# A low score product padded from 64 to 128 rows, in a two-block fp32 kernel

## The chip, the cores and the metric

The kernel runs on one core of one Trainium2 chip. The metric is the device time of one launch in microseconds (us), taken as the median of several runs. All tables of weights are laid out on the host beforehand, without arithmetic, and every product, norm and softmax runs on the core.

## The reference, cut to what matters

The reference is two transformer blocks over 1024 tokens of width 1024, all in fp32. The first block has a sliding-window attention and a gated FFN. The second block has two attentions side by side, and the change sits in the scores of both:

```
# stick-breaking attention, 8 heads of width 64
z = einsum('bhqd,bhkd->bhqk', q, k) * scale          # masked to s < t
log_1mb = where(mask, log_sigmoid(-z), 0)
a = where(mask, exp(log_sigmoid(z) + reverse_cumsum(log_1mb) - log_1mb), 0)
out = a @ v

# differential attention, 4 heads, two score maps of width 64 each
p1 = softmax(where(mask, q1 @ k1.T * scale, -1e30))
p2 = softmax(where(mask, q2 @ k2.T * scale, -1e30))
out = (p1 - lam * p2) @ v
```

After the attentions come gates, a projection with a residual, and a second gated FFN.

## The kernel before, in words

**Precision.** Each fp32 operand is split into a high part, rounded to the format that TensorE takes in one pass (fp32r), and a low part, the rest. A product of two split operands is three products that add up in one PSUM tile: high by high, high by low, low by high. Low by low is left out.

**Scores.** A head of width 64 fills only half of TensorE's 128 rows, so the kernel stacks. `k_stack` (line 1702) loads k's high part into 64 partitions of a tile and k's low part into the other 64. `q_stack` (line 1710) fills a tile `qs` of two slots, for 256 query positions: slot 0 holds q's high part twice, once in each half; slot 1 holds q's low part, in that half alone in which k's high part lies. `scores` (line 1719) then needs two products: slot 0 against all 128 rows of k's tile (line 1723, high by high and high by low at once), and slot 1 against the 64 rows of k's high part (line 1726, low by high). Where the piece touches the diagonal, a third product adds the mask (line 1729). Here q is what is loaded into the array as weights (128 columns of one query tile), and k streams through it, 128 to 512 columns wide.

A stick-breaking call of `scores` handles one pair of q and k. A differential call handles the two score maps together: line 1723 twice, line 1726 twice, line 1729 twice. The second map has its halves swapped (`up` is 1), so that its line 1726 uses rows 64 to 127 while the first map's uses rows 0 to 63.

**The order of the work.** A head's queries come in 8 tiles of 128, and its keys, up to the diagonal, in one or two pieces of at most 512 columns: 12 units for a head, so 96 stick-breaking units and 48 differential ones. Each unit is a tick of a plan written out by hand (`Plan.run`, line 187 on). A stick-breaking unit's scores stand in tick t, its softplus, exponentials and running sum on ScalarE (ACT) and VectorE (DVE) in t+1 and t+2, its transposes on TensorE (line 1735) in t+2, the split of the transposed weights (lines 296 and 297, tile `phl`) in t+3, and its product with v (line 1836) in t+4. A differential unit follows the same pattern (its product with v is line 1976). Between these, `Fill.run` (line 128 on) puts in the projections of the second block and its gates, as products of 512 columns (line 152). Their weights come through SyncE's (SP's) one DMA queue, are rounded on ACT or DVE and split on DVE or GpSimd (POOL, line 102). Every engine works through its own list in order; the lists' order does not depend on what happens at run time.

`q_stack` is called in the slot "load" of a tick, 3 ticks ahead of the tile's first use in a stick-breaking head and 2 ticks ahead in a differential one. The tile `qs` has 4 buffers; there are 64 loads of it, 32 for each attention, three DMAs each.

Of the kernel before, what the change touches and what calls it, by code (L numbers as in the profile page):

```python
# [10 lines left out]
F32 = mybir.dt.float32  # L11
# [183 lines left out]
class Kern:  # L195
# [1401 lines left out]
    def block2_attn(self, stack):  # L1597
        nc = self.nc
# [111 lines left out]
        def q_stack(Q, j, g, cs, up=0):  # L1710

            dst = self.t(pl, [P, 2, 256], "qs", bufs=4, dt=F32R)
            r = slice(g * 64, g * 64 + 64)
            nc.sync.dma_start(dst[:64, 0].bitcast(F32), Q[j][r, cs])
            nc.sync.dma_start(dst[64:, 0].bitcast(F32), Q[j][r, cs])
            nc.sync.dma_start(dst[up * 64 : up * 64 + 64, 1].bitcast(F32), Q[4 + j][r, cs])
            return dst

        def scores(qk, c0, w, mask):

            z = [self.ps("sc")[:, :w] for _ in qk]
            for i, (q, k) in enumerate(qk):
                nc.tensor.matmul(z[i], q[:, 0], k[:, c0 : c0 + w], start=True, stop=False)
            for i, (q, k) in enumerate(qk):
                r = slice(i * 64, i * 64 + 64)
                nc.tensor.matmul(z[i], q[r, 1], k[r, c0 : c0 + w], start=False, stop=mask is None)
            if mask is not None:
                for x in z:
                    nc.tensor.matmul(x[:, w - P : w], self.conr["ident"], self.conr[mask], start=False, stop=True)
            return z  # L1730
# [33 lines left out]
        def stick_head(h):  # L1764
# [21 lines left out]
            for qt in range(NT):  # L1786
                L = (qt + 1) * P
                if qt % 2 == 0:
                    def loadq(qt=qt):
                        H["q", qt] = H["q", qt + 1] = q_stack(SQ, j, g, slice(qt * P, qt * P + 256))  # L1790
                    if h + qt:
                        at(max(0, len(ticks) - 3), "load", loadq)
                    else:
                        loadq()
                for c0, w in reversed(cut(L)):
                    stick_unit(H, h, qt, c0, w, L)

        def stick_unit(H, h, qt, c0, w, L):
# [4 lines left out]
            def score():  # L1803
                q = H["q", qt][:, :, (qt % 2) * P : (qt % 2) * P + P]
                (u["z"],) = scores([(q, H["k"])], c0, w, "stm" if c0 + w == L else None)
# [52 lines left out]
        def diff_head(h):  # L1858
            H = {}

            def load():
                needs(44)
                for s in range(2):
                    H["k", s] = k_stack(DK, h, s, s)
                for i in range(2):
                    H["v", i] = self.t(pl, [P, T], "kv", bufs=6, dt=F32R)
                    nc.sync.dma_start(
                        H["v", i].bitcast(F32), DV[h][:, i * 4 : i * 4 + 4, :].rearrange("p t d -> p (t d)"))

            at(len(ticks) - 5, "load", load)  # L1870
            for qt in range(NT):
                L = (qt + 1) * P
                if qt % 2 == 0:
                    def loadq(qt=qt):
                        for s in range(2):
                            H["q", qt, s] = H["q", qt + 1, s] = q_stack(DQ, h, s, slice(qt * P, qt * P + 256), s)
                    at(len(ticks) - 2, "load", loadq)
                diff_tile(H, h, qt, cut(L), L)
# [62 lines left out]
        def diff_unit(H, Q, t, qt, ch, nch, c0, w, L):  # L1941
            u = {}

            def score():
                qk = [(H["q", qt, s][:, :, (qt % 2) * P : (qt % 2) * P + P], H["k", s]) for s in range(2)]
                u[0], u[1] = scores(qk, c0, w, "dam" if c0 + w == L else None)
# [402 lines left out]
```

## Time and profile before

| what | value |
|---|---|
| median of 3 runs | 2677.01 us (2676.76 to 2686.59) |
| the profiled execution: its time | 2672.5 us |
| the profiled execution: first to last instruction (span) | 2670.7 us |
| PE (TensorE) busy | 2597.1 us, 97% of the span |
| DVE busy | 1870.3 us, 70% |
| ACT busy | 1158.2 us, 43% |
| POOL busy | 660.9 us, 25% |
| mean granted TensorE clock | 0.99 |

A busy PE in this profile is not a PE at its peak: matmuls overlap, and their ends are modelled. What one of them costs is read from the distance between the starts of two that follow each other. The second block's attentions run from about 1154 us to 1800 us of the span.

### The profile page before, as it was taken

How to read it: one execution, taken by the hardware profiler on the slowest of the kernel's cores; microseconds unless marked ns; L12 is line 12 of the kernel's file. 1: busy time of each engine (PE TensorE's matmuls, PEld its weight loads, DVE VectorE, ACT ScalarE, POOL GpSimd, SP SyncE). 2: the span in 40 equal slices, each digit the busy share in tenths (PEclk: the TensorE clock that was granted, in tenths of full speed). 3: DMA queues.
4: the chain of work that ended last, by engine and by line, in shares of the span. 5: the costliest groups of instructions: out<-in, count | busy, mean ns of one | idle time of the engine just before them, and what ended most of it. 6: DMA issues, size and time to landing. Idle time of an engine off the chain costs nothing. (4 is left out here: it accounts for less than half of the span.)

```text
span 2670.7 us, 34280 instructions
## 1 busy us (share of the span) xinstructions
PE 2597.1 (97%) x12078; PEld 2085.7 (78%) x12078; DVE 1870.3 (70%) x2836; ACT 1158.2 (43%) x2080; POOL 660.9 (25%) x571
## 2 busy tenths in 40 slices
PE   9999999999999999899999999999999999999999
PEld 8766787788778778677777777787887788887887
DVE  5688867887887566726788777775636767776654
ACT  3444525433333334526766765554316222323442
POOL 4323254002343332311255111110001003331501
PEclk8999999999999999999999999999999999999999
DMA  6243575434555886346344343336634446565973
GB/s 257 80 158 123 162 264 193 175 137 169 200 171 192 301 285 216 126 128 198 92 131 126 123 132 116 112 105 230 240 142 144 158 140 209 171 215 189 369 243 133
DMA packets 224604, 470.84 MB, mean 176 GB/s; under 512 B 26672, under 2 KB 73904, under 8 KB 224432
## 3 DMA queue, kind: packets, MB, share of 16 engines
q1 hardware_dynamic: 224432, 468.65, 52.3%
q8 instruction: 95, 1.56, 0.2%
q14 instruction: 77, 0.63, 0.1%
HBM read 331.18 MB, written 137.36 MB: 175 GB/s over the span
## 5 line engine op out<-in xcount | busy, mean ns | idle before, releaser
L1353 POOL TENSOR_TENSOR raw<-raw,raw 128x512 f32<-128x512 f32 x78 | 141.3, 1811 | 417.0 <-DMA raw<-in_w_down 210.8
L152 PE MATMUL mm<-ah,wh 128*128 128x512 f32 x544 | 219.8, 404 | 1.8 <-DVE gb L606 1.8
L152 PE MATMUL mm<-ah,wl 128*128 128x512 f32 x544 | 219.3, 403 | 0.0
L152 PE MATMUL mm<-al,wh 128*128 128x512 f32 x544 | 219.0, 403 | 0.0
L102 POOL TENSOR_TENSOR wl<-raw,wh 128x1024 fp32r<-128x1024 f32 x44 | 106.5, 2421 | 399.3 <-DVE wh L101 159.8
L1216 DVE TENSOR_TENSOR W<-W 128x1024 f32<-128x1024 f32 x132 | 129.9, 987 | 14.5 <-DMA W<-in_w_up 12.5
L152 PEld LDWEIGHTS mm<-ah,wh 128*128 128x128 f32 x544 | 102.6, 189 | 22.5 <-issue 2.6
L152 PEld LDWEIGHTS mm<-ah,wl 128*128 128x128 f32 x544 | 102.6, 189 | 20.7 <-issue 2.5
L152 PEld LDWEIGHTS mm<-al,wh 128*128 128x128 f32 x544 | 102.7, 189 | 20.1 <-issue 2.2
L152 PE MATMUL mm<-wl,ah 128*128 128x512 f32 x256 | 102.4, 400 | 1.0 <-DVE wl L102 0.8
L152 PE MATMUL mm<-wh,al 128*128 128x512 f32 x256 | 103.2, 403 | 0.0
L152 PE MATMUL mm<-wh,ah 128*128 128x512 f32 x256 | 102.3, 400 | 0.0
L1152 PE MATMUL sc<-s,wh 128*128 128x512 f32 x344 | 100.6, 394 | 1.6 <-DVE u L1288 1.5
L1820 DVE TENSOR_TENSOR_SCAN w<-sc,w,w 128x383 f32<-128x383 f32 (+3 forms) x96 | 97.4, 1015 | 3.4
L297 DVE TENSOR_TENSOR wl<-rb,wh 128x1024 fp32r<-128x1024 f32 x52 | 77.1, 1483 | 23.7 <-ACT wh L296 19.4
L1507 PE MATMUL sc<-wh,ah 128*128 128x512 f32 x272 | 91.2, 389 | 0.0
L297 DVE TENSOR_TENSOR phl<-tp,phl 128x512 fp32r<-128x512 f32 (+2 forms) x144 | 78.3, 544 | 15.6 <-ACT phl L296 15.5
L1152 PE MATMUL mm<-ah,wh 128*128 128x512 f32 x236 | 79.7, 400 | 8.8 <-DVE wt L1105 5.0
L1816 DVE SCALAR_TENSOR_TENSOR w<-sc,w 128x384 f32<-128x384 f32 (+3 forms) x96 | 53.2, 554 | 45.7 <-ACT w L1815 45.4
L296 ACT CAST phl<-tp 128x512 fp32r<-128x512 f32 (+2 forms) x144 | 67.9, 472 | 34.5 <-PE tp L1735 34.2
L244 POOL TENSOR_SCALAR rs<-ss 128x1 f32<-128x1 f32 x40 | 16.5, 413 | 264.4 <-ACT xn L312 243.3
L1152 PE MATMUL mm<-al,wh 128*128 128x512 f32 x236 | 77.9, 399 | 3.9 <-ACT s L1172 3.9
(561 smaller groups left out, 7603.9 us busy)
## 6 DMA issues: line engine op xcount, KB each, us to landing
W<-in_w_up SPq DMA_DIRECT2D x88, 512.0 KB, 4.5
adaw<-in_ada_w SPq DMA_DIRECT2D x64, 256.0 KB, 3.0
raw<-in_w_in SPq DMA_DIRECT2D x31, 512.0 KB, 3.7
Fa<-g SPq DMA_DIRECT2D x44, 256.0 KB, 2.6
Fb<-g SPq DMA_DIRECT2D x44, 256.0 KB, 2.9
tw<-in_w_down SPq DMA_DIRECT2D x20, 512.0 KB, 5.3
rb<-in_w_down SPq DMA_DIRECT2D x40, 256.0 KB, 5.3
raw<-Fa SPq DMA_DIRECT2D x18, 512.0 KB, 4.9
```

Source lines behind the costliest of these rows:

```text
L102: (nc.vector if i in self.vec else nc.gpsimd).tensor_tensor(out=wl, in0=raw, in1=wh.bitcast(F32), op=ALU.subtract)
L152: kern.last_mm = kern.nc.tensor.matmul(ps, l, r, start=k == 0 and i == 0, stop=k == KT - 1 and i == 2)
L244: self.nc.gpsimd.tensor_scalar(out=out, in0=ss, scalar1=1.0 / n, scalar2=EPS, op0=ALU.mult, op1=ALU.add)
L296: nc.scalar.copy(h, src)
L297: nc.vector.tensor_tensor(out=l, in0=src, in1=h.bitcast(F32), op=ALU.subtract)
L1152: self.last_mm = nc.tensor.matmul(ps, l, r, start=first and k == 0 and i == 0, stop=last and k == 3 and i == 2, skip_group_check=True)
L1216: sub = lambda out, x, y: nc.vector.tensor_tensor(out=out, in0=x, in1=y, op=ALU.subtract)
L1353: eng.tensor_tensor(out=q[out], in0=q[x], in1=q[y], op=op)
L1507: self.last_mm = nc.tensor.matmul(bank, l, r, start=opens and i == 0 and j == 0, stop=closes and i == n - 1 and j == 2, skip_group_check=True)
L1816: nc.vector.scalar_tensor_tensor(out=ls, in0=z, scalar=0.0, in1=ls, op0=ALU.min, op1=ALU.subtract)
L1820: nc.vector.tensor_tensor_scan(out=sg[:, : w - 1][:, ::-1], data0=z[:, 1:w][:, ::-1], data1=ls[:, : w - 1][:, ::-1], initial=sg[:, w - 1 : ...
```

## The change

`q_stack` gets one more instruction: a memset on POOL that sets the unused half of slot 1 to zero. `scores` then multiplies slot 1, all 128 rows of it, with all 128 rows of k's tile. The rows that are new in that product are zeros times k's low part.

```diff
@@ q_stack
             nc.sync.dma_start(dst[64:, 0].bitcast(F32), Q[j][r, cs])
+            nc.gpsimd.memset(dst[64 - up * 64 : 128 - up * 64, 1].bitcast(F32), 0.0)
             nc.sync.dma_start(dst[up * 64 : up * 64 + 64, 1].bitcast(F32), Q[4 + j][r, cs])
@@ scores
             for i, (q, k) in enumerate(qk):
-                r = slice(i * 64, i * 64 + 64)
-                nc.tensor.matmul(z[i], q[r, 1], k[r, c0 : c0 + w], start=False, stop=mask is None)
+                nc.tensor.matmul(z[i], q[:, 1], k[:, c0 : c0 + w], start=False, stop=mask is None)
```

No product is added and none is taken away; TensorE's list has the same products in the same order. Its list at the first stick-breaking unit (`sc` the score tile, `kv` the stacked k, `qs` the stacked q, `mm` a projection of the fill), before:

```order
L152 MATMUL mm_9529<-wh_9495,ah_9298 128x512
L1723 MATMUL sc_9561<-kv_9467,qs_9470 128x128 [waits DMAHW3_49,DMAHW4_49,DMAHW2_49,DMAHW1_49]
L1726 MATMUL sc_9561<-kv_9467,qs_9470 128x128 [waits DMAHW5_49]
L1729 MATMUL sc_9561<-r_stm_74,r_ident_73 128x128
L152 MATMUL mm_9529<-wl_9496,ah_9298 128x512
```

and after:

```order
L152 MATMUL mm_9530<-wh_9496,ah_9298 128x512
L1724 MATMUL sc_9563<-kv_9467,qs_9470 128x128 [waits DMAHW3_49,DMAHW4_49,DMAHW2_49,DMAHW1_49]
L1726 MATMUL sc_9563<-kv_9467,qs_9470 128x128 [waits DMAHW5_49,Pool_49]
L1729 MATMUL sc_9563<-r_stm_74,r_ident_73 128x128
L152 MATMUL mm_9530<-wl_9497,ah_9298 128x512
```

The places are the same; the low product also waits for POOL now, that is, for the memset. (Lines after the new one have moved by one: 1723 is 1724 after the change, and the low product is line 1726 in both.)

POOL's list in the middle of the stick-breaking heads, before (`wl` the low part of the fill's weights, `drs` and `dqn` the norm of the differential q):

```order
L102 TENSOR_TENSOR wl_10229<-raw_9918,wh_10228 128x1024 [waits DMAHW1_49,DVE_49,PE_49]
L102 TENSOR_TENSOR wl_10633<-raw_10232,wh_10632 128x1024 [waits DMAHW3_49,DVE_49,PE_49]
L244 TENSOR_SCALAR drs_10937<-dss_10935 128x8 [waits DVE_49]
L245 TENSOR_TENSOR drs_10937<-drs_10937,mhalf_78 128x8 [waits Pool_49]
L1661 TENSOR_TENSOR dqn_10940<-dqn_10940,cols_69 128x512 [waits DVE_49]
```

and after:

```order
L102 TENSOR_TENSOR wl_10234<-raw_9921,wh_10233 128x1024 [waits DVE_49,DMAHW1_49,PE_49,Pool_49]
L1716 MEMSET qs_10295 64x256 [waits DMAHW7_49,DMAHW0_49,Pool_49]
L1716 MEMSET qs_10380 64x256
L1716 MEMSET qs_10538 64x256 [waits DMAHW4_49,PE_49]
L102 TENSOR_TENSOR wl_10641<-raw_10237,wh_10640 128x1024 [waits DVE_49,DMAHW3_49,PE_49,Pool_49]
L1716 MEMSET qs_10705 64x256 [waits DMAHW7_49,DMAHW0_49,Pool_49]
L1716 MEMSET qs_10787 64x256 [waits DMAHW7_49,DMAHW5_49,DMAHW4_49]
L1716 MEMSET qs_10877 64x256 [waits DMAHW5_49,DMAHW6_49,DMAHW4_49,PE_49]
L244 TENSOR_SCALAR drs_10948<-dss_10946 128x8 [waits DVE_49,Pool_49]
L245 TENSOR_TENSOR drs_10948<-drs_10948,mhalf_78 128x8 [waits Pool_49]
L1661 TENSOR_TENSOR dqn_10951<-dqn_10951,cols_69 128x512 [waits DVE_49]
```

POOL's list grows by 64 memsets of 64 partitions by 256 elements, one for each load of `qs`. Some of them wait for PE, which must have read the buffer's earlier content, and for the DMAs that wrote that content. DVE's and ACT's lists are the same as before, and SP's list has the same DMAs in the same order. On SP the first DMA of a reused `qs` buffer now also waits for POOL, for the memset of the buffer's earlier content.

## Rows read from the trace of the kernel before

**Rows 1.** The page: span, and busy time of each engine.

```profile
span 2670.7 us, 34280 instructions
...
PE 2597.1 (97%) x12078; PEld 2085.7 (78%) x12078; DVE 1870.3 (70%) x2836; ACT 1158.2 (43%) x2080; POOL 660.9 (25%) x571
```

**Rows 2.** Busy time by stretch: stick-breaking heads, differential heads. Times in us.

```profile
core 0: us, PE busy (x) PEld busy (x) DVE busy (x) ACT busy (x) POOL busy (x), PEclk, DMA share, GB/s
...
1213.00:1580.00 367.00, 358.92 (x1775) 275.81 (x1774) 292.18 (x556) 256.13 (x551) 113.06 (x157) 1.00 0.42 128
1580.00:1800.00 220.00, 218.99 (x1202) 173.19 (x1202) 167.90 (x432) 116.69 (x369) 30.25 (x23) 1.00 0.37 111
```

**Rows 3.** PE's waits, 1150 to 1805 us: total, times, longest.

```profile
PE sc L1723 <- DMA qs<-sqh: 3.9, 2, 2.4
PE tp L1735 <- DVE phl L297: 3.5, 4, 1.4
```

**Rows 4.** Line 1726: duration in ns (min/median/max), first and last start, forms.

```profile
L1726 PEld LDWEIGHTS sc<-kv,qs x192: 182/183/183, 1155.0 to 1795.3; 64*128 64x128 f32 x192
L1726 PE MATMUL sc<-kv,qs x192: 322/441/502, 1155.0 to 1795.3; 64*128 64x384 f32 x80, 64*128 64x512 f32 x64, 64*128 64x256 f32 x32, 64*128 64x128 f32 x16
```

**Rows 5.** Timeline, PE, two stick-breaking units: start us, duration us, engine, line.

```profile
1292.05 0.30 PE L1723 MATMUL sc<-kv,qs 128*128 128x128 f32 x1
...
1292.70 0.45 PE L152 MATMUL mm<-wh,al 128*128 128x512 f32 x1
...
1570.30 0.48 PE L1723 MATMUL sc<-kv,qs 128*128 128x512 f32 x1
...
1570.71 0.50 PE L1726 MATMUL sc<-kv,qs 64*128 64x512 f32 x1
1571.15 0.33 PE L1729 MATMUL sc<-r_stm,r_ident 128*128 128x128 f32 x1
...
1571.31 0.44 PE L152 MATMUL mm<-ah,wl 128*128 128x512 f32 x1
...
1571.59 0.39 PE L152 MATMUL mm<-ah,wh 128*128 128x512 f32 x1
...
1571.82 0.39 PE L152 MATMUL mm<-al,wh 128*128 128x512 f32 x1
```

**Rows 6.** Timeline, PE, two differential units.

```profile
1700.31 1.08 PE L1976 MATMUL po<-kv,phl 128*128 128x256 f32 x8
1701.23 0.63 PE L1723 MATMUL sc<-kv,qs 128*128 128x512 f32 x2
1701.79 0.50 PE L1726 MATMUL sc<-kv,qs 64*128 64x512 f32 x2
1702.22 0.44 PE L1729 MATMUL sc<-r_dam,r_ident 128*128 128x128 f32 x2
1702.50 0.45 PE L152 MATMUL mm<-al,wh 128*128 128x512 f32 x1
...
1706.80 0.52 PE L1723 MATMUL sc<-kv,qs 128*128 128x384 f32 x2
...
1707.62 0.50 PE L152 MATMUL mm<-ah,wh 128*128 128x512 f32 x1
```

**Rows 7.** Timeline, split weights (DVE) and their product with v, two units.

```profile
1432.42 0.53 DVE L297 TENSOR_TENSOR phl<-tp,phl 128x384 fp32r<-128x384 f32 x1
...
1441.59 0.67 DVE L297 TENSOR_TENSOR phl<-tp,phl 128x512 fp32r<-128x512 f32 x1
...
1435.28 0.52 PE L1836 MATMUL po<-phl,kv 128*128 128x256 f32 x3
...
1442.36 0.69 PE L1836 MATMUL po<-phl,kv 128*128 128x256 f32 x4
```

**Rows 8.** POOL's groups by form: busy us, mean ns, idle before.

```profile
L102 POOL TENSOR_TENSOR wl<-raw,wh 128x1024 fp32r<-128x1024 f32 x27 | 64.8, 2403 | 339.2 <-DVE wh L101 159.8 <-issue 93.3 <-PE tp L1735 35.4
...
L451 POOL MEMSET ra<- 128x256 f32 x1 | 0.3, 312 | 0.0
```

**Rows 9.** The DMAs of the low part of q, line 1716, from issue to landing.

```profile
DMA to landing us min/median/max: 2.2/2.4/6.8
```

## The prediction

> **What bounds the kernel now.** I read the page first: TensorE (PE) is busy for 97% of the span, no other engine for more than 70% [rows 1]. I then asked for busy times in the stretch that the change touches. From 1213 to 1580 us, the stick-breaking heads, PE is busy 358.9 of 367 us and DVE 292.2, that is 80%; from 1580 to 1800 us, the differential heads, PE is busy 219.0 of 220 us, and DVE 76% [rows 2]. The granted clock is 1.00 in both, the higher of its two levels (2.4 GHz), so it has nothing to give. PE's waits from 1150 to 1805 us are eight rows of 3.9 us and less, some 13 us in all, and the two largest are the first loads of q and the transposes behind DVE's split [rows 3]. So PE's own list sets the time here: a microsecond taken from PE between 1154 and 1800 us is a microsecond of the end, as long as DVE and ACT keep up.
>
> "Busy" hides what the products cost, so I went by starts. Two products of 512 columns that follow each other in the fill start 0.23 us apart (1571.59 and 1571.82) [rows 5]. Around line 1726 the distances are longer. In a stick-breaking unit of 512 columns with a mask, line 1726 starts 0.41 us after line 1723, where 0.23 would be usual; the next product starts 0.44 us after line 1726, where again 0.23 would be usual; and the mask's small product holds its follower off by 0.16 us [rows 5]. So a product over 64 rows between products over 128 rows costs about 0.18 us when it is entered and 0.21 us when it is left.
>
> **The change part by part.** *Stick-breaking units, the low product over 128 rows.* There are 192 low products [rows 4], 96 of them here: 12 units for each of 8 heads, of which 64 (one for each query tile) carry a mask. If a product over 128 rows behind another follows at the pitch of the fill, an unmasked unit saves 0.18 + 0.21 = 0.39 us. For the masked unit I also need the pitch of narrow products: eight products of lines 1976 run from 1700.31 to 1701.23 us, 0.115 us each [rows 6], each with weights of its own, so I take 0.115 us as the floor for a narrow one. The masked unit then goes from 1.01 us (1570.30 to 1571.31) to 0.23 + 0.23 + 0.115 = 0.575, a saving of 0.43. A unit of 128 columns goes from 0.65 us (1292.05 to 1292.70) [rows 5] to three floors, 0.345, a saving of 0.305. The sum is 32 x 0.39 + 56 x 0.43 + 8 x 0.305 = 12.5 + 24.1 + 2.4 = 39 us. The 56 masked units include widths of 256 and 384; that the two extra distances don't depend on the width is an assumption, which the next part's row at 384 columns bears out.
>
> *Differential units.* Here a saving and a cost meet. The two low products of a unit use different halves of the rows and run side by side: the pair covers 0.50 us [rows 6], as long as the single one of a stick-breaking unit [rows 5]. A unit of 512 columns takes 1.27 us from its first score product to the next fill product (1701.23 to 1702.50) [rows 6]. After the change the four products stand in a row: 4 x 0.23 + 2 x 0.115 for the masks = 1.15, a saving of only 0.12 us. At 384 columns without a mask it is 0.82 us (1706.80 to 1707.62) [rows 6] against 4 x 0.173 = 0.69, a saving of 0.13, with the pitch scaled by columns. The masks alone go from 0.28 us (1702.22 to 1702.50) to 0.23, so 0.07 is left for 512 without a mask, and 0.18 comes out for 384 with one. From both sizes the drains of a unit are worth 0.30 us and the lost pairing one pitch; for 256 and 128 columns that gives 0.30 - 0.115 + 0.05 = 0.235. With 8 masked and 8 unmasked units of 512, 12 and 8 of 384, 8 masked of 256 and 4 of 128: 1.0 + 0.6 + 2.2 + 1.0 + 1.9 + 0.9 = 7.5; I take 7, since the 128-column ones will hardly reach it.
>
> The Trainium skill speaks against this edit in "TensorEngine Tiling (Array Packing)", section "When to Use Tiling": a contraction of 64 or less is a case for splitting the array by rows, for up to twice the speed. The trace shows that only for the differential pairs; a stick-breaking unit has one product and nothing to pair it with. The rule alone, without the entry and exit that the rows show, would make the change a loss (the fourth case below).
>
> *The memset.* 64 memsets of 64 x 256 elements. The nearest row is one of 128 x 256 at 0.312 us [rows 8]; the elements of one partition are as many, so I take 0.31 us each, 20 us of POOL's time over 587 us, of which it is idle for three quarters [rows 2]. On PE's path this costs nothing as long as the memset lands before the DMA that it stands beside: the same call issues the low part's DMA, which takes a median of 2.4 us to land [rows 9], and both wait for the same release of the buffer. What stands behind a memset on POOL are the fill's splits (line 102), which run up to four units of weights ahead, and the norms of the differential q and k, which have ten to 24 fill products of room. Bounds: nothing on PE's path below (and no gain); above, 20 us, were POOL's time a delay of PE one for one. I take 0, as the cover is wide.
>
> *What gets late next.* When PE moves faster, its products with v and its transposes meet DVE and ACT earlier. DVE is busy 292 us in a stretch that shrinks from 367 to about 328 us: 89%, not yet a bound, but a chain with less slack. I looked at that slack. Usually the split is done 2 to 4 us before PE wants it (the one that begins at 1432.42 ends at 1432.95, its product starts at 1435.28), but once in each head, where two pieces of 512 columns follow each other, there is next to none (1441.59 + 0.67 = 1442.26, product at 1442.36) [rows 7]. Four units' savings, 4 x 0.39 = 1.6 us, lie between a score and its product with v, so at such a place up to 1.6 us turns into a wait: 8 x 1.6 = 13 us at most in the first places, some 3 more in the units behind them, 0 at least, if DVE and ACT move up as far as PE (they get their scores earlier too). I take 10.
>
> *Sum:* 39 + 7 - 0 - 10 = 36 us. The profiled execution took 2672.5 us with a span of 2670.7; 2672.5 - 36 = 2636.5. The median of the runs, 2677.0, stands 4.5 us above the profiled one, so I predict 2641.
>
> **The rivals.**
>
> *B: the chain over ACT and DVE becomes the bound in the stick-breaking heads.* For it: DVE's 80%, the place without slack in each head, and PE's present waits on the split. Against it: slack of whole microseconds elsewhere. If half of the 39 us goes, 39/2 + 7 = 26 are left, 2651; if all of it goes, 2670.
>
> *C: a weight load cannot run beside a product any more.* The Trainium skill says in "TensorE: Matmul & The Clock Gate", section "The mechanism", that a weight load overlaps products in flight only where it goes to other rows of the array. By that, all 192 low products would now wait for a load on the rows in use. With the load's 0.183 us [rows 4] that is 35 us back, 46 - 35 = 11, 2666. Against it: eight products with eight loads at 0.115 us each [rows 6], and fill products at 0.23.
>
> *D, the slower one: PE waits for the memset.* The low product of each tile now waits for POOL, and POOL works in order. If each memset stood behind one of the fill's splits (2.4 us [rows 8]) that had itself just been let go, PE would wait up to 2.4 us at 64 places: 154 - 46 = 108 us slower, 2785. It decides from 46/64 = 0.7 us of wait at each tile. Against it: loads stand two or three ticks ahead, and the DMA needs 2.4 us anyway.
>
> *E: the change doesn't do what it says.* The 0.18 and 0.21 us might come from adding into the tile that was just written, not from the number of rows. Then nothing goes, and the differential pairs lose their overlap: 16 x 0.23 + 20 x 0.173 + 12 x 0.115 = 8.5 us, 2686. Against it: fill products add into one tile at 0.23 us [rows 5].
>
> **How the numbers follow.** The forecast has 0.72, B 0.15, C 0.03, D 0.04, E 0.06. From 0.5% on, 13.4 us (below 2663.6 or above 2690.4), a difference can be told from none. Faster: the forecast and four fifths of B, 0.84. Slower: D, 0.04. The rest, 0.12, is the same (the end of B, C, E). The range begins at 2629, where nothing is lost to the chain (2677 - 46 = 2631) and a little more comes off the entries than I read, and ends at 2662, which takes in the forecast with the 16 us of lost slack (2647) and most of B.
>
> **What would show it.** Line 1726's starts should follow line 1724's at 0.23 us for 512 columns, and the next product at 0.23; the pairs of a differential unit should start one pitch apart. The stretch of the stick-breaking heads should be about 30 us shorter and that of the differential heads about 7. PE's waits on DVE's split and on ACT should rise to some 15 to 20 us, and none should name the memset. The rest of the span should keep its length. I am wrong if the distances around line 1726 stay (E), if they shrink and PE waits instead for DVE (B), for its own weights (C), or for POOL (D).

## The result

The changed kernel takes 2642.8 us in the median (2639.0 to 2643.4) against 2677.2 of before: the ratio is 0.985, with a 95% interval from 0.983 to 0.987. The forecast was 2641 in a range from 2629 to 2662. A later comparison of the same two kernels, in another job, gave 2632.9 against 2680.4, ratio 0.983 (0.981 to 0.985). The forecast's size holds. PE's two terms came out together as forecast, though not from the parts that I had put them together from; the third term, what the chain over ACT and DVE takes back, was too large. The time outside the stretch that the change touches varies by some 10 us, so the closeness to the first median is partly luck.

The page of the profile after, span and busy time, answers to [rows 1]:

```profile
span 2641.1 us, 34532 instructions
...
PE 2562.3 (97%) x12078; PEld 2098.1 (79%) x12078; DVE 1868.8 (71%) x2836; ACT 1157.2 (44%) x2080; POOL 673.3 (25%) x635
```

PE has the same 12078 products and 34.8 us less of busy time; POOL has 64 instructions and 12 us more. The busy time by stretch, the heads' two parts as in [rows 2]:

```profile
core 0: us, PE busy (x) PEld busy (x) DVE busy (x) ACT busy (x) POOL busy (x), PEclk, DMA share, GB/s
1220.00:1560.00 340.00, 326.03 (x1771) 272.24 (x1770) 289.85 (x556) 255.33 (x551) 123.05 (x190) 0.99 0.46 138
1560.00:1771.00 211.00, 209.80 (x1209) 182.42 (x1209) 167.88 (x432) 116.26 (x370) 38.71 (x51) 1.00 0.39 117
```

The stretch of the stick-breaking heads went from 367 to 340 us and that of the differential heads from 220 to 211. DVE does the same work in less time: 85% busy in the first of them, where it was 80%. The first score product now stands at 1162.7 us of the span, 8 us later than in the profiled execution of before. That is ahead of anything the change touches, and a later execution of the changed kernel has it at 1157.7. TensorE's clock goes with it: up to the first low product it stood at its lower level for 48 us in the profile of before, 55 in that later one and 60 in this one. So the two profiled spans differ by 29.6 us only, while the stretch from the first low product to the last lost 37.

The timeline of PE in two stick-breaking units of 512 columns, the first without and the second with a mask, answers to [rows 5] (line 1723 is 1724 here):

```profile
1548.17 0.49 PE L1724 MATMUL sc<-kv,qs 128*128 128x512 f32 x1
1548.49 0.39 PE L1726 MATMUL sc<-kv,qs 128*128 128x512 f32 x1
1548.72 0.39 PE L152 MATMUL mm<-ah,wh 128*128 128x512 f32 x1
1548.95 0.40 PE L152 MATMUL mm<-al,wh 128*128 128x512 f32 x1
...
1551.86 0.47 PE L1724 MATMUL sc<-kv,qs 128*128 128x512 f32 x1
1552.18 0.39 PE L1726 MATMUL sc<-kv,qs 128*128 128x512 f32 x1
1552.41 0.22 PE L1729 MATMUL sc<-r_stm,r_ident 128*128 128x128 f32 x1
1552.46 0.45 PE L152 MATMUL mm<-ah,wl 128*128 128x512 f32 x1
1552.75 0.40 PE L152 MATMUL mm<-ah,wh 128*128 128x512 f32 x1
```

An unmasked unit of the kernel before, to set beside the first:

```profile
1574.71 0.47 PE L1723 MATMUL sc<-kv,qs 128*128 128x512 f32 x1
1575.12 0.50 PE L1726 MATMUL sc<-kv,qs 64*128 64x512 f32 x1
1575.55 0.50 PE L152 MATMUL mm<-ah,wl 128*128 128x512 f32 x1
1575.88 0.40 PE L152 MATMUL mm<-ah,wh 128*128 128x512 f32 x1
```

The product after line 1726 now follows at 0.23 us, the fill's pitch. But line 1726 itself follows line 1724 after 0.32 us, where I had expected 0.23. To the product behind it, the masked unit takes 0.60 us, where it took 1.01, and the unmasked one 0.55, where it took 0.84. In the kernel before the unmasked unit costs something behind that as well: the fill product that follows line 1726 is itself followed after 0.33 us (1575.55 to 1575.88), not 0.23. Measured to this second product, the unmasked unit goes from 1.17 to 0.78 us and the masked one from 1.29 (1570.30 to 1571.59 [rows 5]) to 0.89. And the differential unit that answers to the first one of [rows 6]:

```profile
1676.56 0.63 PE L1724 MATMUL sc<-kv,qs 128*128 128x512 f32 x2
1677.03 0.62 PE L1726 MATMUL sc<-kv,qs 128*128 128x512 f32 x2
1677.49 0.33 PE L1729 MATMUL sc<-r_dam,r_ident 128*128 128x128 f32 x2
1677.66 0.44 PE L152 MATMUL mm<-al,wh 128*128 128x512 f32 x1
```

The pair of low products covers 0.62 us, no longer 0.50: it doesn't run side by side any more. The unit still went from 1.27 to 1.10 us. Added up over all units, from the first score product to the second product behind the unit, the 96 stick-breaking ones went from 109.1 to 74.7 us and the 48 differential ones from 63.5 to 53.6. (To the first product behind the unit it is 79.8 to 47.2 and 49.0 to 40.8, which misses the late second product behind the unmasked units.)

PE's waits from 1150 to 1805 us, the four largest of nine rows, answer to [rows 3]:

```profile
PE tp L1735 <- DVE phl L297: 4.5, 5, 1.4
PE sc L1724 <- DMA qs<-sqh: 4.0, 1, 4.0
PE po L1836 <- DVE phl L297: 3.6, 3, 2.0
PE mm L152 <- POOL wl L102: 1.8, 3, 1.1
```

The nine rows add up to 19 us, 6 more than before. None names the memset. POOL's group of memsets, to which the one of [rows 8] answers:

```profile
L1716 POOL MEMSET qs<- 64x256 f32 x64 | 19.4, 310 | 67.1 <-PE sc L1726 33.5 <-DMA sql<-u 19.8 <-PE sc L1729 6.1
```

0.310 us each, as the row of another memset had said. POOL does stand still for 33.5 us until PE has read an old buffer, and that costs nothing, as the kernel with the memsets alone shows below.

### The profile page after: what moved, and what is told of

It is laid out like the page before. It is cut to its first block, busy times and chain, and to the rows that moved or that the text cites. A ratio compares the mean times of both kernels' runs of the same rounds, so it can differ in the third digit from the quotient of the medians.

```text
span 2641.1 us, 34532 instructions
## 1 busy us (share of the span) xinstructions
PE 2562.3 (97%) x12078; PEld 2098.1 (79%) x12078; DVE 1868.8 (71%) x2836; ACT 1157.2 (44%) x2080; POOL 673.3 (25%) x635
## 4 chain that ended last, share of the span: by engine, by line
PE 61%; DVE 8%; DMA 5%; ACT 3%; issue 3%; POOL 2%; SPq 0%; DVEq 0%; POOLq 0%; ACTq 0%
PE sc L1152 14%; PE mm L152 13%; PE mm L1152 5%; PE sc L1507 5%; PE po L1152 4%; PE mm L1507 3%; PE tp L1507 3%; PE tp L1735 2%; PE po L1507 1%; PE po L1976 1%; PE sc L1724 1%; PE sc L1726 1%; PE po L1836 1%; PE mm L266 1%; PE mm L265 1%
## 5 line engine op out<-in xcount | busy, mean ns | idle before, releaser
L258 ACT CAST wh<-raw 128x1024 fp32r<-128x1024 f32 x41 | 42.8, 1049 | 83.3 <-PE mm L267 64.4
L1253 DVE SCALAR_TENSOR_TENSOR g<-gp,cols,g 128x512 f32<-128x512 f32 x88 | 75.9, 882 | 4.1 <-ACT g L1250 2.4
```

What stands on the lines that cost most here:

```text
L258: nc.scalar.copy(wh, raw)
L1253: nc.vector.scalar_tensor_tensor(out=g, in0=G.gp[:, o + tap : o + tap + HALF], scalar=fcw[:, i : i + 1], in1=g, op0=ALU.mult, op1=ALU.add)
```

## The experiments

**One attention at a time, and the memset alone.** The first kernel pads for the stick-breaking heads only, the second for the differential heads only, each with the memsets of those heads; the third issues all the memsets but keeps the products at 64 rows. The products' edit of all three in one:

```diff
-                nc.tensor.matmul(z[i], q[:, 1], k[:, c0 : c0 + w], start=False, stop=mask is None)
+                r = slice(0, P) if len(qk) == 1 else slice(i * 64, i * 64 + 64)   # first; second: len(qk) == 2
+                r = slice(i * 64, i * 64 + 64)                                     # third
+                nc.tensor.matmul(z[i], q[r, 1], k[r, c0 : c0 + w], start=False, stop=mask is None)
```

> Padding (and its memset) in the stick-breaking heads alone; the differential heads keep their 64-row products. Theory S (what goes is the cost of entering and leaving a 64-row product): the stretch of the stick-breaking heads, 424 us before and 397 after, is 397 here, that of the differential heads stays at 216, and the time is 27 us below before: 2650. If the two parts don't add up, because the stick-breaking heads' chain over ACT and DVE only got its slack from elsewhere (theory B), less: 2655 to 2665.

> Padding in the differential heads alone. Theory S: four products in a row without a switch against three pitches and a switch, 8 us less on PE, a stretch of 206 us in place of 216; time 2667 to 2669. Rival (row tiling wins where two products run side by side, and no switch costs anything): the pairs lose their overlap, 8.5 us more, 2686.

> The 64 memsets alone; all low products over 64 rows as before. Theory S with a hidden memset: 2677, as before, and no wait of PE names the memset. Rival D (POOL's time reaches PE): up to 64 x 0.31 = 20 us slower, 2697, and more if PE waits for the memset itself.

Measured: 2648.9 us (ratio 0.989, 0.987 to 0.990), 2668.0 us (0.996, 0.994 to 0.997) and 2680.6 us (1.000, 0.999 to 1.002), beside a median of 2680.2 for before. The shares, 1.15% and 0.43%, add up to 1.6%, where the whole change gave 1.5% and 1.7% in its two comparisons: the parts add up, and the memset costs nothing. The low products' first and last starts (in us, behind the durations in ns), in the stick-breaking and then the differential heads, tell it without the parts of the span that vary. The changed kernel:

```profile
L1726 PE MATMUL sc<-kv,qs x96: 274/340/522, 1162.9 to 1556.2; 128*128 128x384 f32 x40, 128*128 128x512 f32 x32, 128*128 128x256 f32 x16, 128*128 128x128 f32 x8
L1726 PE MATMUL sc<-kv,qs x96: 273/337/396, 1559.9 to 1766.4; 128*128 128x384 f32 x40, 128*128 128x512 f32 x32, 128*128 128x256 f32 x16, 128*128 128x128 f32 x8
```

Padding in the stick-breaking heads alone:

```profile
L1728 PE MATMUL sc<-kv,qs x96: 274/340/412, 1156.6 to 1547.5; 128*128 128x384 f32 x40, 128*128 128x512 f32 x32, 128*128 128x256 f32 x16, 128*128 128x128 f32 x8
L1728 PE MATMUL sc<-kv,qs x96: 323/440/503, 1551.3 to 1767.3; 64*128 64x384 f32 x40, 64*128 64x512 f32 x32, 64*128 64x256 f32 x16, 64*128 64x128 f32 x8
```

Padding in the differential heads alone:

```profile
L1728 PE MATMUL sc<-kv,qs x96: 323/442/686, 1157.3 to 1580.9; 64*128 64x384 f32 x40, 64*128 64x512 f32 x32, 64*128 64x256 f32 x16, 64*128 64x128 f32 x8
L1728 PE MATMUL sc<-kv,qs x96: 273/337/397, 1585.0 to 1791.3; 128*128 128x384 f32 x40, 128*128 128x512 f32 x32, 128*128 128x256 f32 x16, 128*128 128x128 f32 x8
```

The memsets alone:

```profile
L1727 PE MATMUL sc<-kv,qs x96: 324/442/683, 1155.8 to 1579.8; 64*128 64x384 f32 x40, 64*128 64x512 f32 x32, 64*128 64x256 f32 x16, 64*128 64x128 f32 x8
L1727 PE MATMUL sc<-kv,qs x96: 323/440/503, 1583.9 to 1799.9; 64*128 64x384 f32 x40, 64*128 64x512 f32 x32, 64*128 64x256 f32 x16, 64*128 64x128 f32 x8
```

From the first to the last low product the differential heads take 216.0 us at 64 rows in both kernels that have them so, and 206.3 and 206.5 at 128: 9.6 us gained. From the first low product of the stick-breaking heads to the first of the differential ones it is 427.7 and 428.1 us at 64 rows (424.3 in the profiled execution of before), 394.7 and 397.0 at 128 (395.0 in the second profile of the changed kernel). The granted clock sorts these: over this stretch it is 1.00 in the profiles with 424.3, 394.7 and 395.0 us, and 0.98 or 0.99 in the three others. At 1.00 the gain is 29.5 us. Of the rivals, E, by which the differential pairs would only have lost their overlap, and the memset (D) fall here.

**Is it the number of rows?** Three of the 24 products in each group of the fill go over 64 rows in the changed kernel; the other 64 rows of these products are left out:

```diff
+                    h = slice(0, 64) if k in (2, 4, 6) and i == 0 else slice(0, P)
-                    kern.last_mm = kern.nc.tensor.matmul(ps, l, r, ...)
+                    kern.last_mm = kern.nc.tensor.matmul(ps, l[h], r[h], ...)
```

> The changed kernel, but three products of 24 in each group of the two attentions' fill go over rows 0 to 63 only (the other 64 rows of those products are left out): 300 more 64-row products, with no transposes ahead of them and no new operand. Theory S: each costs one entry and one exit, 0.10 + 0.20 = 0.30 us, 90 us in all where PE is the bound: about 2725. Rival E (the distances come from adding into the tile just written, or from the low operand, not from the number of rows): 2643, nothing changes.

Measured: 2728.6 us, 86 above the changed kernel's first median and 96 above its later one, for 300 products over half as many rows. The timeline shows where (line 153 is the fill's product):

```profile
1401.04 0.40 PE L153 MATMUL mm<-wl,ah 128*128 128x512 f32 x1
1401.27 0.40 PE L153 MATMUL mm<-wh,al 128*128 128x512 f32 x1
1401.60 0.49 PE L153 MATMUL mm<-wh,ah 64*128 64x512 f32 x1
1402.02 0.49 PE L153 MATMUL mm<-wl,ah 128*128 128x512 f32 x1
1402.36 0.64 PE L1837 MATMUL po<-phl,kv 128*128 128x256 f32 x4
```

From 128 rows to 128 it is 0.23 us, from 128 to 64 0.33, from 64 to 128 0.42, and from there to the next product 0.34: 0.10 to enter, 0.19 to leave, and 0.11 more behind the next product, 0.40 us in all. Set beside the same places of the changed kernel's later trace, the 154 products that stand among fill products cost 0.40 us each, and all 300 together 107 us of PE's distances. PE's waits fell at the same time, from 20.7 us (1150 to 1820 us, changed kernel) to 9.0 (1150 to 1890 us here), which leaves about the 96 us by which the time rose. So the expectation's 90 us was met, but by a price that was too small and waits that it didn't count.

The weight loads (PEld) show the same change of rows. In the kernel before, the loads of line 1726 and of the mask's product behind it, in the masked unit of [rows 5]:

```profile
1570.71 0.18 PEld L1726 LDWEIGHTS sc<-kv,qs 64*128 64x128 f32 x1 [0.25 <-issue]
1571.14 0.19 PEld L1729 LDWEIGHTS sc<-r_stm,r_ident 128*128 128x128 f32 x1 [0.25 <-issue]
```

In the changed kernel, in its masked unit above:

```profile
1551.39 0.48 PEld L1735 LDWEIGHTS tp<-cons,w 128*128 128x128 f32 x3
1551.84 0.19 PEld L1724 LDWEIGHTS sc<-kv,qs 128*128 128x128 f32 x1
1551.95 0.19 PEld L1726 LDWEIGHTS sc<-kv,qs 128*128 128x128 f32 x1
```

At 128 rows the load of line 1726 begins 0.23 us ahead of its product (1552.18); at 64 rows it begins with its product (1570.71), after 0.25 us in which no load runs, and so does the load behind it. Over all 192 low products the loads stood idle ahead of line 1726 for 25.5 us in 105 places before, and for none in the changed kernel's first profile.

The Trainium skill names a cause in "TensorEngine Tiling (Array Packing)", section "Key Properties": changing the tiling mode drains TensorE. The trace agrees, as far as loads that no longer run ahead and 0.40 us for each lone product can show a drain. By this experiment the cause is the number of rows, whatever the operands.

**Whose are the other 0.08 us?** In a stick-breaking unit the transposes of another unit stand right ahead of the scores. Here they stand ahead of the last batch of fill products instead, once in the kernel before and once in the changed one:

```diff
-            n + 8, ("load", "A", "A2", "B", "B2", "C0", "C", 0, "D0", "D", "F", 1, "G"), fill[0],
+            n + 8, ("load", "A", "A2", "B", "B2", "C0", "C", 0, "D0", "D", "F", "G", 1), fill[0],
```

> The kernel before, with a tick's transposes put ahead of the last batch of fill products in place of behind it, so that a unit's scores follow a fill product and not transposes; nothing else moves. Theory S with its corrected size (entry 0.10 us; another 0.08 us ahead of line 1726 belongs to the transposes that come just before line 1723): line 1726 of a stick-breaking unit of 512 columns starts 0.32 to 0.33 us after line 1723, not 0.41, and the fill product behind the transposes is followed after 0.32 us, not 0.23. As predicted at first (entry 0.18 us): 0.41 stays. Time as before, 2677 to 2682, or a little more from waits on ACT.

> The same move of the transposes in the changed kernel. Theory S: line 1726 starts 0.23 us after line 1724 at 512 columns in place of 0.31, the 0.08 us go to the fill product behind the transposes, and the sum does not change: 2643, up to 5 us more where the transposes now wait for ACT's last exponential.

Measured: 2693.3 us in a single run, and 2648.7 us (ratio to before 0.988, 0.986 to 0.991). In the kernel before with this move, the fill's products behind the transposes, and then a unit of 384 columns:

```profile
1570.69 0.47 PE L152 MATMUL mm<-ah,wl 128*128 128x512 f32 x1
1571.01 0.39 PE L152 MATMUL mm<-ah,wh 128*128 128x512 f32 x1
1571.24 0.39 PE L152 MATMUL mm<-al,wh 128*128 128x512 f32 x1
...
1571.70 0.33 PE L1723 MATMUL sc<-kv,qs 128*128 128x384 f32 x1
1571.97 0.44 PE L1726 MATMUL sc<-kv,qs 64*128 64x384 f32 x1
1572.34 0.50 PE L152 MATMUL mm<-ah,wh 128*128 128x512 f32 x1
```

The product behind the transposes holds its follower off for 0.32 us, and the entry is 0.27 us, 0.10 above the 0.17 that 384 columns take. At 512 columns, the width of the expectation, the median over the 32 units is 0.33, where it was 0.41. In the changed kernel with the move:

```profile
1551.39 0.39 PE L1724 MATMUL sc<-kv,qs 128*128 128x512 f32 x1
1551.63 0.39 PE L1726 MATMUL sc<-kv,qs 128*128 128x512 f32 x1
1551.85 0.39 PE L152 MATMUL mm<-ah,wh 128*128 128x512 f32 x1
```

Line 1726 follows at 0.24 us. So 0.08 of the 0.18 us that I had put down to the entry belong to the transposes and stay, wherever these stand.

The weight loads say more. The transposes' three loads take 0.48 us, and the load of line 1724 behind them begins only 0.02 us ahead of its product (1551.84 and 1551.86), where most fill products' loads begin 0.23 us ahead. In the trace of the kernel before, from 1150 to 1800 us, the products of 512 columns over 128 rows that are followed without a wait by another over 128 rows can be sorted by how far ahead their load begins. The median time to the next product's start, for all groups of more than three, is:

| load begins ahead by, us | products | to the next start, us |
|---|---|---|
| 0.00 | 51 | 0.34 |
| 0.03 | 58 | 0.32 |
| 0.06 | 96 | 0.28 |
| 0.11 to 0.12 | 110 | 0.23 |
| 0.22 to 0.24 | 1345 | 0.23 |

So a load that begins less than about 0.1 us ahead goes with a late follower, whatever delayed it: the change of rows (0.00), the transposes (0.03) or the mask's product (0.06). No run varies the load alone.

The move itself costs time: 11 us over the job's median in the kernel before (one run), and in the changed kernel 6 us over its first median, where I had allowed up to 5. PE now meets ACT and DVE one batch of fill products earlier. Its largest wait in the changed kernel with the move:

```profile
PE tp L1735 <- DVE phl L297: 13.9, 11, 3.6
```

That is 4.5 us without it.

**What does the chain over DVE still take?** Two kernels take work from DVE or POOL, and a third does both:

```diff
-        fill.append(Fill(self, srcs, nc.vector.tensor_copy, products, (0, 1, 2, 3, 11, 13, 15, 17, 19, 21)))
+        fill.append(Fill(self, srcs, nc.vector.tensor_copy, products, (0, 1, 2, 3)))         # splits moved
+        fill.append(Fill(self, srcs, nc.vector.tensor_copy, products, (0, 1, 2, 3, 13, 17, 21)))   # in the third
-            nc.gpsimd.memset(dst[64 - up * 64 : 128 - up * 64, 1].bitcast(F32), 0.0)
-            nc.sync.dma_start(dst[up * 64 : up * 64 + 64, 1].bitcast(F32), Q[4 + j][r, cs])
+            nc.sync.dma_start(dst[:64, 1].bitcast(F32), Q[4 + j][r, cs])              # low part twice
+            nc.sync.dma_start(dst[64:, 1].bitcast(F32), Q[4 + j][r, cs])
```

> The changed kernel, with six more of the fill's splits on POOL in place of DVE. Theory B (the chain over DVE takes back part of the gain, 10 us as predicted): some of PE's waits on DVE's split and on the head's output go, 3 to 6 us faster, 2637 to 2640. If the chain takes back next to nothing: 2643, within 2 us.

> The changed kernel without the memset: the other half of slot 1 gets q's low part too, by a fourth DMA, so the product over 128 rows adds low by low as well. If the memset is hidden and SP's queue has room, 2643, as the changed kernel; if POOL's 20 us had cost something, up to 5 us less; if 64 more DMAs hold up SP's queue, more.

> The changed kernel with the low part in both halves of slot 1 (no memset) and three more of the fill's splits on POOL in place of DVE. If the chain over DVE still takes back some 3 us and POOL's own splits were late only because six moved at once: 2637 to 2640, 3 to 6 us below the changed kernel run beside it. If what is left of PE's waits doesn't hang on DVE's load: as the changed kernel, within 2 us.

> The changed kernel once more, unedited, on the same chip as the run before it, to compare the two and to see how far the stretch ahead of the second block's attentions varies from one execution to the next. 2643, within 5 us; the stretch of the stick-breaking heads 395 to 397 us, that of the differential heads 206.

Measured, as ratios to before: splits moved 2639.0 us, 0.985 (0.983 to 0.987); low part twice 2641.7 us, 0.986 (0.984 to 0.989); both 2641.3 us, 0.986 (0.984 to 0.988); the changed kernel beside it 2632.9 us, 0.983 (0.981 to 0.985). All the intervals overlap, and the last one lies 10 us from its own expectation of 2643, where 5 were allowed. So no version here is shown to beat the changed kernel. The first one's 2639.0 us falls where its expectation put "the chain still takes something", but that decides nothing beside a changed kernel at 2632.9; and the third came out 8 us above the changed kernel of its own job, where its expectation had 3 to 6 below or the same. The stretch shows no gain from moving the splits either: in the first one the stick-breaking heads take 400.4 us from low product to low product (1158.7 to 1559.1) at a granted clock of 0.98, against 397.0 at 0.99 and 395.0 at 1.00 in the changed kernel. The second one also shows that the zeros don't matter for the time: there the new rows hold q's low part. The waits say why moving the splits gains nothing; PE's first and fourth largest with six of them on POOL:

```profile
PE mm L152 <- POOL wl L102: 7.5, 5, 3.0
...
PE tp L1735 <- DVE phl L297: 1.9, 3, 1.1
```

What PE no longer waits for DVE, it waits for POOL. The changed kernel's second profile repeats the stretches, 395.0 us to the first differential low product and 206.4 from there to the last:

```profile
L1726 PE MATMUL sc<-kv,qs x96: 273/340/412, 1158.1 to 1549.3; 128*128 128x384 f32 x40, 128*128 128x512 f32 x32, 128*128 128x256 f32 x16, 128*128 128x128 f32 x8
L1726 PE MATMUL sc<-kv,qs x96: 273/337/409, 1553.1 to 1759.5; 128*128 128x384 f32 x40, 128*128 128x512 f32 x32, 128*128 128x256 f32 x16, 128*128 128x128 f32 x8
```

Most of the 14.1 us between the two profiled spans come from outside: the first low product stands 4.8 us earlier, and the span ends at 2627.0 us, 867.5 after the last low product, where it was 874.7 in the first profile (2641.1 - 1766.4). The clock differs there too: behind the last low product it stood at its lower level for 7 us in the first profile and not at all in the second. What lowers it in one execution and not in the next was not tried, nor whether it explains all of the difference.

## Why the prediction was right, point by point

- **The bound.** Right: most of what went from PE's list between 1154 and 1800 us went from the end.
- **The stick-breaking units, 39 us.** The mechanism is right, and the size nearly so, partly by luck. To the second product behind it, a unit saved 0.39 us at the median, masked or not, at every width from 256 columns on, and 0.29 us at 128: 88 x 0.39 + 8 x 0.29 = 37 us. The forecast had 0.39 for an unmasked unit, 0.43 for a masked one and 0.305 at 128. But its 0.39 was 0.18 for entering and 0.21 for leaving, and the runs show 0.10 and 0.20, and 0.10 behind the next product. The other 0.08 of the entry belong to the transposes, and the 0.10 behind the next product was overlooked; the two nearly cancel. In the masked unit the 0.16 us behind the mask's product had taken the late part in, and the floor of 0.115 was too high for that distance (0.05 us now), so that the two didn't cancel there.
- **The differential units, 7 us.** Measured 9.9 us on PE's distances and 9.6 in the stretch. The pairing was lost as expected and the drains paid for it; they are worth 0.40 us a unit and not the 0.30 that I worked out, since the unmasked unit was measured to the first product behind it and the two masks together cost 0.17 us now (1677.49 to 1677.66), not 0.23.
- **The memset, 0.** Right, 0.31 us each and hidden, shown by the kernel with the memsets alone (ratio 1.000) and by the one without them.
- **The chain over ACT and DVE, 10 us back.** Too large. The stretch gained 29.5 us of PE's 37, so some 7 came back, all of it in the stick-breaking heads; PE's nine waits rose by 6 us over both attentions, to 19. The part of them that I had named, DVE's split and ACT, is 9.7 us and not the 15 to 20 that I expected. That the places without slack get part of the gain too, since their scores come earlier, I had named and then counted as little; why so little is lost was not tested.
- **The sum.** 46 - 10 = 36 was forecast. On PE it was 37 + 10 = 47, and some 39 us in the two stretches. The medians differ by 34.4 us in the first comparison and by 47.5 in the second, with what varies outside. So the sum of PE's terms and the path are confirmed; that 2641 lies within 2 us of the first median is partly luck.
- **The rivals.** B took some 7 us, not half of 39. C fails: in the padded unit the load of line 1726 begins at 1551.95 us, while line 1724's product over the same rows, begun at 1551.86, still runs, and the next product follows line 1726 at the fill's pitch, 0.23 us. That is against the rule of the Trainium skill in "TensorE: Matmul & The Clock Gate", section "The mechanism", which has loads overlap products only on other rows. D and E fail as told.

## What to carry to other kernels

A single product over half the rows between products over all of them pays for entering and leaving, here 0.40 us, nearly two whole products of 512 columns; zeros in the other half are cheaper, even where two such products could run side by side but make only one pair. When a distance between two starts is put down to a cause, look for the same distance in a place where another neighbour stands ahead: here that would have taken the transposes' share out of the entry before the sum was made. And follow the starts behind the place until the usual pitch is back: the last 0.10 us of this price stand one product further on. And when an edit takes work from the bound, read the next bound from its slack place by place, but count that what feeds it comes earlier too.

## What the runs showed of the hardware beyond that

The product that follows transposes of 128 columns is itself followed 0.08 us later than usual (0.32 us in place of 0.23), with a fill product as with a score product, and the trace of the kernel before has the late starts go with weight loads that begin late (the table above). And the time outside the edited stretch differs by some 10 us between executions of the same kernel (12 us between the two profiles of the changed one, with 6 and 7 us more of the lower clock level ahead and behind), so that an edit of this size is better read from the stretch than from the span.
